# The low-rank gates of the odd layer: three 16-bit parts in one product of 96 rows, in place of rounded 4-byte parts in one of 80 rows

## The chip, the cores and the metric

The kernel runs on one core of one Trainium2 chip. The metric is the device time of one execution in microseconds; lower is better. The engines are called by the profile's names: PE is TensorE (PEld its weight loads), DVE is VectorE, ACT is ScalarE, POOL is GpSimd, and SP is SyncE, which here only issues DMAs.

## The reference, cut to what matters

One inference step of a decoder with two layers, for a prompt of 2048 tokens and 32 sample tokens (8 sequences of 4). Layer 0 has two head groups beside each other, a gated linear recurrence and a forgetting attention. Layer 1, the odd layer, is gated linear attention with four heads. Every layer ends with an output projection that is added to the input. What the change touches is the decay gate of the odd layer:

```python
proj = h @ w_in                                  # 1024 -> q 512, k 512, v 1024, g 1024, r 16
q, k, v, g, r = _split(proj, [...])
log_f = jax.nn.log_sigmoid((r @ w_gate + b_gate).astype(jnp.float32)) / GLA_GATE_NORMALIZER
...
o, s = gated_linear_chunked(hk(q) * C_KEY_DIM ** -0.5, hk(k), hv(v), hk(log_f), gla_s0)
```

The gate has rank 16: r has 16 columns per token, w_gate is 16 x 512, and each of the four heads uses 128 of the 512 columns. All inputs and outputs are float32.

## The kernel before, in words

Large projections are made with operands split in two float16 parts, high and low, and three products (`mm3`, lines 626 to 628: high x high, high x low, low x high). The tokens are worked off in two halves of 1024, the first with the 32 sample tokens behind it. A *unit* is a block of up to 272 output columns. For each unit the weights are loaded by SP into `wr_...`, measured, scaled by a power of two and split into `w_...` (`half_unit`, lines 338 to 366: L356 and L362/L363 on ACT, L357 on DVE, L364 on POOL); then the unit's own generator runs.

For each half of the odd layer there are three units a head: `mk_v` (values, and with head 0 the 16 columns of r), `mk_qk` (q, k and the gate), `mk_g` (the output gate). Beside the units of the next head or half runs `lin_attn` of the head before: the recurrence in levels of doubling width, with short products `gl_C` (L757) on PE, products of q, k and the running decay f on DVE (L789, L791) and POOL (L790), the sample tokens' step (`decode`, L796 to L846), and the outer products (`o_C`, `kt_C`). `mux` interleaves two generators in the program by costs written in the code. In the order that results, a scheduler of the framework (`schedule_with_timeline_sim=True`) then places the instructions of every engine's queue and gives tiles their buffers. `issue_after` adds an order without data.

The 16 columns of r take this way. In `mk_v` of head 0, for each group of 128 tokens (eight a half, and one of 32 in the first half), `ev` gets the projection in PSUM. ACT copies the values out (L1911). DVE makes `rh`, r scaled and rounded to the matrix engine's 4-byte format (L1920), copies it four times into `rt` (L1921) and puts the remainder in a fifth block of 16 columns (L1922). Two groups later `flip` transposes `rt` on PE into the PSUM tile `prT` (L1926), and DVE copies that into `rT` (L1927), 80 rows by 1024 or 1056 tokens. In `mk_qk`, `gate` multiplies the weights `wg` with `rT` in pieces of 352 columns (first half) or 512 (second) into the tile `zC` (L1951), 20 products in all, which ACT (L1953) and DVE (L1954) read.

`wg` is made once, in `more_consts`, which is placed early in the even layer (some 50 to 76 us into the span): a memset (L199), three loads of the same 16 rows to rows 0, 32 and 64 (L201), one rounding copy on ACT (L203), one subtraction on DVE (L204). The raw tile comes from the tag `y`, with three buffers, of which the tile `lb` (the even layer's lower bound, L175 to L194) also takes one, and out of which the five masks `mtmp` are made after it: a memset and two selects on POOL (L211, L213, L215) and four small casts on DVE each (L219). The first state loads of `lin_attn` (`s_A`, L830) use the same tag. In the same stretch the weights of the unit `Aqf` are scaled and split; L292 is the DVE instruction that reads a unit's maximum from the PSUM tile `spr_...` into `pow_...`.

Of the kernel before, what the change touches and what calls it, by code (L numbers as in the profile page):

```python
# [8 lines left out]
F32 = mybir.dt.float32  # L9
F32R = mybir.dt.float32r  # L10
BF16 = mybir.dt.bfloat16
# [3 lines left out]
AF = mybir.ActivationFunctionType  # L15
ALU = mybir.AluOpType
# [3 lines left out]
P = 128  # L20
# [3 lines left out]
HALF = 1024  # L24
DB, DS = 8, 4
TS = DB * DS
# [45 lines left out]
def as32(ap):  # L72

    return ap if ap.dtype == F16 else ap.bitcast(F32)
# [51 lines left out]
class Kern:  # L126
# [40 lines left out]
    def more_consts(self, mp):  # L167
        nc, i, cp, col = self.nc, self.i, self.cp, self.col
# [7 lines left out]
        l0, l1, m = (lb[:, r * NH : (r + 1) * NH] for r in range(3))  # L176
# [18 lines left out]
        self.bgla = col("bgla", i["b_gla_gate"][0], NH)  # L195


        wg = mp.tile([P, 512], F32, tag="y", name="wgr")
        nc.vector.memset(wg[:80], 0.0)  # L199
        for r in (0, 32, 64):  # L200
            nc.sync.dma_start(wg[r : r + 16], i["w_gla_gate"][0])  # L201
        self.wg = cp.tile([80, 512], F32R, name="wg")
        nc.scalar.activation(self.wg, wg[:80], AF.Copy)  # L203
        nc.vector.tensor_tensor(self.wg[32:48], wg[32:48], as32(self.wg[32:48]), ALU.subtract)  # L204
        self.bfox = cp.tile([P, NH], F32, name="bfox")
        nc.sync.dma_start(self.bfox, i["b_fox_f"].to_broadcast([P, NH]))

# [25 lines left out]
        for g in range(3):  # L233
            m = self.rowmask[g * TS : (g + 1) * TS]
# [1645 lines left out]
    def odd_half(self, hf, act, wpool, wp, pps, S):  # L1880
        nc, i, o = self.nc, self.i, self.o
        w = i["w_in_odd"][0]
        n = self.ncols(hf)
        q, f, k, v, vs, sg = {}, {}, {}, {}, {}, {}
        rTs = {}
        if hf == 0:
            self.q_undo = [self.kcol() for _ in range(NH)]

        def c4(nm):
            return wp.tile([P, HALF + TS], F32, tag="c4", name=nm)  # L1890

        def unit(n, h, run):
            nm, cols = self.odd_cols(h)[n]
            return (self.half_unit(wpool, pps, w, cols, f"{nm}{h}", f"{nm}{hf}{h}"), run)

        def undo(nm):
            return self.scales[nm][:, 2:3]

        def mk_v(h):
            width = 272 if h == 0 else 256  # L1900

            def run(W):
                v[h] = wp.tile([P, 8, 256], F32, tag="v8", name=f"vC{hf}{h}")
                vs[h] = wp.tile([TS, 256], F32, tag="vs", name=f"vsC{hf}{h}")
                if h == 0:
                    rTs[0] = wp.tile([80, HALF + TS], F32R, tag="rT", name=f"rT{hf}")

                def ev(ps, g, cnt, m):
                    c = undo(f"Cv{h}")[:m]
                    if m == P:  # L1910
                        r = nc.scalar.activation(v[h][:, g : g + cnt], ps[:, :, :256], AF.Copy, scale=c)  # L1911
                        if h == 0:
                            self.last_ev = r
                    else:
                        nc.scalar.activation(vs[h], ps[:, 0, :256], AF.Copy, scale=c)
                    if h == 0:
                        rt = wp.tile([P, 5, 16], F32, tag="rt", name=f"rt{hf}{g}")
                        rh = wp.tile([P, 16], F32R, tag="rh", name=f"rh{hf}{g}")
                        r = ps[:, 0, 256:272]
                        nc.vector.tensor_scalar(rh[:m], r, c, None, ALU.mult)  # L1920
                        nc.vector.tensor_copy(rt[:m, :4], as32(rh[:m]).unsqueeze(1).to_broadcast([m, 4, 16]))  # L1921
                        nc.vector.scalar_tensor_tensor(rt[:m, 4], r, c, as32(rh[:m]), ALU.mult, ALU.subtract)  # L1922

                        def flip():
                            pr = pps.tile([P, 512], F32, tag=PRT[hf], name=f"prT{hf}{g}")
                            nc.tensor.transpose(pr[:80, :m], rt[:m].rearrange("p a b -> p (a b)"), self.ident[:m, :m])  # L1926
                            nc.vector.tensor_copy(rTs[0][:, g * P : g * P + m], pr[:80, :m])  # L1927

                        if len(waiting) > 1:
                            waiting.pop(0)()  # L1930
                        waiting.append(flip)

                waiting = []
                yield from self.proj_tm(pps, act, W, hf, ev, f"Cv{hf}{h}", width)
                for x in waiting:
                    x()

            return unit(0, h, run)

        def mk_qk(h):  # L1940
            def run(W):
                nm = f"C{hf}{h}"

                def gate():
                    f[h], u = c4("f" + nm), c4("u" + nm)
                    ff = f[h]
                    for x, (c0, m) in enumerate(self.segs(hf)):
                        if x and h == 0:
                            yield
                        ps = pps.tile([P, 512], F32, tag="pj", name=f"z{nm}{c0}")  # L1950
                        nc.tensor.matmul(ps[:, :m], self.wg[:, h * P : (h + 1) * P], rTs[0][:, c0 : c0 + m],  # L1951
                                         start=True, stop=True)
                        nc.scalar.activation(ff[:, c0 : c0 + m], ps[:, :m], AF.Abs, bias=self.bgla[:, h : h + 1])  # L1953
                        nc.vector.tensor_scalar(u[:, c0 : c0 + m], ps[:, :m], self.bgla[:, h : h + 1], 0.0,  # L1954
                                                ALU.add, ALU.min)
                    nc.scalar.activation(ff[:, :n], ff[:, :n], AF.Exp, scale=-1.0)
                    nc.scalar.activation(ff[:, :n], ff[:, :n], AF.Ln, bias=1.0)
                    nc.vector.tensor_tensor(ff[:, :n], u[:, :n], ff[:, :n], ALU.subtract)
                    nc.scalar.activation(ff[:, :n], ff[:, :n], AF.Exp, scale=1.0 / 16)

                q[h], k[h] = c4("q" + nm), c4("k" + nm)
                c = undo(f"Cqk{h}")
                if hf == 0:
                    nc.vector.tensor_scalar(self.q_undo[h], c, SCALE, None, ALU.mult)
                yield from self.proj_fm(pps, act, W, 0, P, hf, lambda ps, c0, m: nc.scalar.activation(
                    q[h][:, c0 : c0 + m], ps, AF.Copy, scale=self.q_undo[h]), nm + "q")
                gates = gate()
                next(gates, None)
                yield Z_C
                for x in self.proj_fm(pps, act, W, P, P, hf, lambda ps, c0, m: nc.scalar.activation(  # L1970
                        k[h][:, c0 : c0 + m], ps, AF.Copy, scale=c), nm + "k"):
                    next(gates, None)
                    yield x

            return unit(1, h, run)

        def mk_g(h):
            def run(W):
                nm = f"C{hf}{h}"
                sg[h] = []  # L1980
                for t in range(2):
                    s = wp.tile([P, HALF + TS], F32, tag="sg", name=f"sg{t}{nm}")
                    sg[h].append(s)
                    yield from self.proj_fm(pps, act, W, t * P, P, hf, lambda ps, c0, m: self.silu2(
                        wp, s[:, c0 : c0 + m], ps, m, f"{nm}{t}{c0}", undo(f"Cg{h}")), f"{nm}g{t}")

            return unit(2, h, run)

        us = []
        for h in range(NH):  # L1990
            us += [mk_v(h), mk_qk(h), mk_g(h)]

        def lin(h):
            return self.lin_attn(wp, pps, hf, h, 256, q[h], f[h], k[h], v[h], vs[h], sg[h],
                                 self.g_gla[:, 2 * h : 2 * h + 2], S[h], i["state_gla"][0, :, h],
                                 o["gla_s"][0, :, h], o["gla_p"][0, 0, h],
                                 [self.yT[1][2 * h + t] for t in range(2)], f"C{hf}{h}")

        return us, lin
# [223 lines left out]
```

## Time and profile before

| | before |
|---|---|
| median of 3 runs | 2328.9 us |
| lowest and highest run | 2323.44 and 2330.65 us |
| profiled execution, its time | 2327.16 us |
| its span, first to last instruction | 2325.5 us |
| granted TensorE clock, mean | 0.991 |
| PE busy | 2251.2 us, 97% of the span |
| DVE, ACT, POOL busy | 1377.3, 1026.8, 727.0 us |

The span is what the trace covers; the execution's time is 1.7 us longer. In a row of the timeline stand the start, the duration, the engine, the line, the operation, the tile written and the tiles read, the shapes and the count; in brackets the time for which the engine was idle before it and what ended that. A row of waits names who waited for whom, then the sum, the number of times and the longest. A row of one tile or one line gives the shortest, median and longest duration in ns, and the first and last start in us. Ends of matmul records are modelled; starts are not. Records of the 4-byte product carry the type f32.

### The profile page before, as it was taken

The numbers are of one execution on the slowest core, as the hardware profiler recorded it, in microseconds if no ns is written. First come the engines' busy times: TensorE is split into PE (matmuls) and PEld (weight loads), VectorE is DVE, ScalarE is ACT, GpSimd is POOL, SyncE is SP. The second block draws the span as 40 slices with busy tenths as digits, with TensorE's granted clock in tenths as the row PEclk, the third lists the DMA queues.
The fourth block names the chain that finished last, engine by engine and source line by source line (L and its number), as shares of the span: only waits on it lengthen the run. The fifth ranks groups of instructions, "written<-read, shape, count | busy, mean of one in ns | idle before, by whom it ended". The sixth has DMA issues, their size and how long they took to land.

```text
span 2325.5 us, 57677 instructions
## 1 busy us (share of the span) xinstructions
PE 2251.2 (97%) x23060; PEld 1605.5 (69%) x23060; DVE 1377.3 (59%) x3074; ACT 1026.8 (44%) x2264; POOL 727.0 (31%) x780
## 2 busy tenths in 40 slices
PE   7999999999999999999999999999999999999998
PEld 5677678855755876655446888777677666666887
DVE  7756558525653657577767455366665655547554
ACT  6434354211212226456656543545544644554343
POOL 2223424001201214123335445144551432222232
PEclk9999999999999999999999999999999999999999
DMA  7343444755432378876972969424224431115553
GB/s 238 121 126 99 146 135 163 206 137 160 143 120 73 124 187 282 236 248 191 274 257 82 343 193 267 130 79 143 82 93 93 124 92 58 49 56 164 171 186 150
DMA packets 357422, 361.63 MB, mean 156 GB/s; under 512 B 105777, under 2 KB 300658, under 8 KB 353058
## 3 DMA queue, kind: packets, MB, share of 16 engines
q1 hardware_dynamic: 355010, 351.33, 49.3%
q0 software_dynamic: 2144, 6.62, 0.8%
q8 instruction: 181, 2.97, 0.5%
q14 instruction: 87, 0.71, 0.1%
HBM read 244.54 MB, written 96.42 MB: 147 GB/s over the span
## 4 chain that ended last, share of the span: by engine, by line
PE 42%; DVE 2%; POOL 2%; ACT 2%; DMA 1%; issue 1%; SPq 0%; POOLq 0%; DVEq 0%; ACTq 0%
PE pt_o L626 4%; PE pt_o L627 4%; PE pt_o L628 4%; PE pt_Cv L626 2%; PE pt_Cv L628 2%; PE pt_Cv L627 2%; PE gl_C L757 1%; PE o_C L910 1%; PE pt L1449 1%; PE pv L1711 1%; DMA yr<-yT 1%; POOL s_C L843 1%; PE py_C L729 1%; POOL kC L790 0%; PE fo L626 0%
## 5 line engine op out<-in xcount | busy, mean ns | idle before, releaser
L626 PE MATMUL pt_o<-w_o,act 128*128 128x256 f16 x1024 | 279.6, 273 | 2.7 <-ACT sg1C L683 2.7
L627 PE MATMUL pt_o<-w_o,act 128*128 128x256 f16 x1024 | 279.7, 273 | 0.0
L628 PE MATMUL pt_o<-w_o,act 128*128 128x256 f16 x1024 | 279.5, 273 | 0.1
L626 PEld LDWEIGHTS <-act 128*128 128x128 f16 x2304 | 226.3, 98 | 37.4 <-issue 3.7
L627 PEld LDWEIGHTS <-act 128*128 128x128 f16 x2304 | 226.4, 98 | 32.9 <-issue 4.2
L628 PEld LDWEIGHTS <-act 128*128 128x128 f16 x2304 | 226.4, 98 | 30.6 <-issue 2.0
L790 POOL TENSOR_TENSOR kA<-kA,fA 128x512 f32<-128x512 f32 (+1 forms) x56 | 77.2, 1378 | 339.5 <-PE gl_A L757 274.5
L626 PE MATMUL pt_Cv<-w_Cv,act 128*128 128x256 f16 (+1 forms) x512 | 141.4, 276 | 0.0
L627 PE MATMUL pt_Cv<-w_Cv,act 128*128 128x256 f16 (+1 forms) x512 | 141.3, 276 | 0.0
L628 PE MATMUL pt_Cv<-w_Cv,act 128*128 128x256 f16 (+1 forms) x512 | 141.3, 276 | 0.0
L1429 POOL TENSOR_SCALAR L<-L,nm 128x512 f32<-128x512 f32 (+3 forms) x160 | 99.3, 634 | 107.7 <-DVE nm L1425 41.5
L1421 ACT ACTIVATE L<-L,nm,kc 128x512 f32<-128x512 f32 (+3 forms) x160 | 118.2, 740 | 27.7 <-DVE nm L1419 26.9
L790 POOL TENSOR_TENSOR kC<-kC,fC 128x512 f32<-128x512 f32 (+1 forms) x56 | 80.2, 1433 | 142.2 <-PE gl_C L757 100.1
L1456 ACT ACTIVATE th<-pt 128x512 f16<-128x512 f32 (+3 forms) x159 | 81.8, 529 | 92.5 <-PE pt L1449 91.1
L1457 DVE TENSOR_TENSOR tl<-pt,th 128x512 f16<-128x512 f32 (+3 forms) x159 | 95.1, 609 | 21.2 <-ACT th L1456 19.5
L1449 PE MATMUL pt<-ident,L 128*128 128x128 f32 x544 | 91.8, 281 | 1.6 <-POOL L L1429 1.0
L1573 PEld LDWEIGHTS pkt<-ident,pgcache_fox_k 128*128 128x128 f32 x512 | 58.3, 141 | 44.0 <-issue 25.1
L789 DVE TENSOR_TENSOR qC<-qC,fC 128x512 f32<-128x512 f32 (+1 forms) x56 | 73.4, 1311 | 23.4 <-PE gl_C L757 23.4
L1449 PEld LDWEIGHTS pt<-ident,L 128*128 128x128 f32 x544 | 67.6, 144 | 26.1 <-DVE tl L1457 5.2
L1573 PE MATMUL pkt<-ident,pgcache_fox_k 128*128 128x128 f32 x512 | 77.7, 278 | 6.8 <-ACT kts L1577 2.5
L1911 ACT ACTIVATE vC<-pt_Cv,kc 128x512 f32<-128x512 f32 (+1 forms) x40 | 23.9, 599 | 136.5 <-PE pt_Cv L628 136.5
L789 DVE TENSOR_TENSOR qA<-qA,fA 128x512 f32<-128x512 f32 (+1 forms) x56 | 70.1, 1253 | 12.5 <-PE gl_A L757 12.4
(959 smaller groups left out, 6558.2 us busy)
## 6 DMA issues: line engine op xcount, KB each, us to landing
pgcache_fox_k<-in_cache_fox_k SPq DMA_DIRECT2D x128, 256.0 KB, 4.2
pgcache_fox_v<-in_cache_fox_v SPq DMA_DIRECT2D x128, 256.0 KB, 4.1
yr<-yT SPq DMA_DIRECT2D x16, 1024.0 KB, 6.8
x1d<-xo SPq DMA_DIRECT2D x44, 256.0 KB, 3.6
wr_o<-in_w_out_even SPq DMA_DIRECT2D x32, 256.0 KB, 5.1
xo<-in_x_prompt SPq DMA_DIRECT2D x32, 256.0 KB, 5.6
wr_Cv<-in_w_in_odd SPq DMA_DIRECT2D x32, 256.0 KB, 3.5
x1r<-x1d SPq DMA_DIRECT2D x16, 512.0 KB, 4.2
```

Source lines behind the costliest of these rows:

```text
L626: nc.tensor.matmul(ps, lh[0], rh[0], start=first, stop=False)
L627: nc.tensor.matmul(ps, lh[0], rh[1], start=False, stop=False)
L628: return nc.tensor.matmul(ps, lh[1], rh[0], start=False, stop=last)
L789: nc.vector.tensor_tensor(xv[:, :, 1], xv[:, :, 1], t0.to_broadcast([P, nb, w]), ALU.mult)
L790: nc.gpsimd.tensor_tensor(kv[:, :, 0], kv[:, :, 0], t1.to_broadcast([P, nb, w]), ALU.mult)
L1421: self.last_exp = nc.scalar.activation(lt[:, :w], lt[:, :w], AF.Exp, bias=nm[:, 0:1], scale=ib, accum_out=nm[:, 2 + j : 3 + j])
L1429: nc.gpsimd.tensor_scalar(lt[:, :w], lt[:, :w], nm[:, 1:2], 2.0**14, ALU.mult, ALU.mult)
L1449: nc.tensor.transpose(pt[:, w : w + P], rows[b][s // 4][0][:, (s % 4) * P : (s % 4 + 1) * P], self.ident)
L1456: nc.scalar.activation(th[:, a:w], pt[:, a:w], AF.Copy),
L1457: nc.vector.tensor_tensor(tl[:, a:w], pt[:, a:w], th[:, a:w], ALU.subtract)))
L1573: last = nc.tensor.transpose(pk[:, j * P : (j + 1) * P], pgs[j][:, h * P : (h + 1) * P], self.ident)
L1911: r = nc.scalar.activation(v[h][:, g : g + cnt], ps[:, :, :256], AF.Copy, scale=c)
```

## The change

Both operands of the gate's product are split into three bfloat16 parts, in place of a rounded part and a remainder. Six blocks of 16 rows, 96 in all, hold the parts 0, 1, 2, 0, 1, 0 of the weights against the parts 0, 0, 0, 1, 1, 2 of r, so that one product sums the six pairs. The weights' parts are made by two ACT copies and two DVE subtractions on 16 rows and are put in place by six DMAs of 16 KB that POOL issues, where before the rows came from HBM three times and were computed in place. For r, DVE makes the high part (16 bits), the remainder, its 16-bit part, three copies of the first and two of the second, and subtracts once more. `rT` holds 16-bit values in a tile of the same size as before.

```diff
@@ more_consts
-        wg = mp.tile([P, 512], F32, tag="y", name="wgr")
-        nc.vector.memset(wg[:80], 0.0)
-        for r in (0, 32, 64):
-            nc.sync.dma_start(wg[r : r + 16], i["w_gla_gate"][0])
-        self.wg = cp.tile([80, 512], F32R, name="wg")
-        nc.scalar.activation(self.wg, wg[:80], AF.Copy)
-        nc.vector.tensor_tensor(self.wg[32:48], wg[32:48], as32(self.wg[32:48]), ALU.subtract)
+        wg, left = (mp.tile([P, 512], F32, tag="y", name=x)[:16] for x in ("wgr", "wgl"))
+        nc.sync.dma_start(wg, i["w_gla_gate"][0])
+        w3 = mp.tile([P, 512], F32, tag="pd", name="wg3")
+        parts = [w3[:16, 0:256].bitcast(BF16), w3[:16, 256:512].bitcast(BF16), mp.tile([P, 512], F32, tag="kt", name="wg1")[
+            :16, :256].bitcast(BF16)]
+        self.wg = cp.tile([96, 512], BF16, name="wg")
+        nc.scalar.activation(parts[0], wg, AF.Copy)
+        nc.vector.tensor_tensor(left, wg, parts[0], ALU.subtract)
+        nc.scalar.activation(parts[1], left, AF.Copy)
+        nc.vector.tensor_tensor(parts[2], left, parts[1], ALU.subtract)
+        for g, x in enumerate((0, 1, 2, 0, 1, 0)):
+            nc.gpsimd.dma_start(self.wg[16 * g : 16 * g + 16], parts[x])
@@ mk_v
-                    rTs[0] = wp.tile([80, HALF + TS], F32R, tag="rT", name=f"rT{hf}")
+                    rTs[0] = wp.tile([P, HALF + TS], F32, tag="rT", name=f"rT{hf}").bitcast(BF16)[:96, : HALF + TS]
...
-                        rt = wp.tile([P, 5, 16], F32, tag="rt", name=f"rt{hf}{g}")
-                        rh = wp.tile([P, 16], F32R, tag="rh", name=f"rh{hf}{g}")
+                        rt = wp.tile([P, 6, 16], F32, tag="rt", name=f"rt{hf}{g}")
+                        rh = wp.tile([P, 2, 16], BF16, tag="rh", name=f"rh{hf}{g}")
                         r = ps[:, 0, 256:272]
-                        nc.vector.tensor_scalar(rh[:m], r, c, None, ALU.mult)
-                        nc.vector.tensor_copy(rt[:m, :4], as32(rh[:m]).unsqueeze(1).to_broadcast([m, 4, 16]))
-                        nc.vector.scalar_tensor_tensor(rt[:m, 4], r, c, as32(rh[:m]), ALU.mult, ALU.subtract)
+                        nc.vector.tensor_scalar(rh[:m, 0], r, c, None, ALU.mult)
+                        nc.vector.scalar_tensor_tensor(rt[:m, 5], r, c, rh[:m, 0], ALU.mult, ALU.subtract)
+                        nc.vector.tensor_copy(rh[:m, 1], rt[:m, 5])
+                        nc.vector.tensor_copy(rt[:m, :3], rh[:m, 0:1].to_broadcast([m, 3, 16]))
+                        nc.vector.tensor_copy(rt[:m, 3:5], rh[:m, 1:2].to_broadcast([m, 2, 16]))
+                        nc.vector.tensor_tensor(rt[:m, 5], rt[:m, 5], rt[:m, 3], ALU.subtract)
 
                         def flip():
                             pr = pps.tile([P, 512], F32, tag=PRT[hf], name=f"prT{hf}{g}")
-                            nc.tensor.transpose(pr[:80, :m], rt[:m].rearrange("p a b -> p (a b)"), self.ident[:m, :m])
-                            nc.vector.tensor_copy(rTs[0][:, g * P : g * P + m], pr[:80, :m])
+                            nc.tensor.transpose(pr[:96, :m], rt[:m].rearrange("p a b -> p (a b)"), self.ident[:m, :m])
+                            nc.vector.tensor_copy(rTs[0][:, g * P : g * P + m], pr[:96, :m])
```

## The prediction

> **What bounds the kernel now.** I read the first part of the page, then the chain that ended last, then TensorE's waits in the odd layer, then busy time in the two stretches in which the changed code runs.
>
> ```profile
> span 2325.5 us, 57677 instructions
> PE 2251.2 (97%) x23060; PEld 1605.5 (69%) x23060; DVE 1377.3 (59%) x3074; ACT 1026.8 (44%) x2264; POOL 727.0 (31%) x780
> PE 42%; DVE 2%; POOL 2%; ACT 2%; DMA 1%; issue 1%; SPq 0%; POOLq 0%; DVEq 0%; ACTq 0%
> ```
>
> TensorE is busy for 97% of the span, and it is the engine with by far the most of the last chain. Work on the other engines costs time only where TensorE waits for it. In the odd layer those waits are few:
>
> ```profile
> PE gl_C L757 <- POOL kC L790: 5.2, 3, 1.8
> PE gl_C L757 <- DVE qC L711: 1.9, 1, 1.9
> PE o_C L626 <- ACT pd_C01s L861: 1.6, 1, 1.6
> PE ktS_C L805 <- DVE kr_C L804: 0.7, 1, 0.7
> PE gl_C L757 <- DVE qC L789: 0.3, 1, 0.3
> 1450.00:1483.00 33.00, 33.00 (x281) 25.48 (x280) 12.12 (x44) 15.85 (x31) 5.03 (x5) 1.00 0.76 192
> 1795.00:1830.00 35.00, 34.00 (x583) 24.12 (x581) 29.70 (x67) 16.85 (x37) 21.07 (x17) 1.00 0.72 174
> ```
>
> The last two rows are the stretches in which the rows of r are made, for the first and the second half of the tokens (columns: PE, PEld, DVE, ACT, POOL busy). In the first VectorE has 21 us free. In the second it has 5.3 us free, because the last head of the first half is worked off beside it, and POOL is busy for 21.07 of 35 us.
>
> **The change, part by part.** *The gate product.* There are twenty products zC, twelve of 352 columns and eight of 512. Their inputs become 16 bits wide and 96 rows deep.
>
> ```profile
> L1951 PEld LDWEIGHTS zC<-rT,wg x20: 186/190/193, 1483.6 to 2076.5; 80*128 80x128 f32 x20
> L1951 PE MATMUL zC<-rT,wg x20: 322/442/587, 1483.6 to 2076.8; 80*128 80x352 f32 x12, 80*128 80x512 f32 x8
> 1483.25 0.31 PE L626 MATMUL pf_C00q<-act,w_Cqk 128*128 128x352 f16 x1
> 1483.40 0.31 PE L627 MATMUL pf_C00q<-act,w_Cqk 128*128 128x352 f16 x1
> 1483.55 0.31 PE L628 MATMUL pf_C00q<-act,w_Cqk 128*128 128x352 f16 x1
> 1483.58 0.45 PE L1951 MATMUL zC<-rT,wg 80*128 80x352 f32 x1
> 1483.87 0.33 PE L626 MATMUL pf_C00k<-act,w_Cqk 128*128 128x352 f16 x1
> 1484.03 0.31 PE L627 MATMUL pf_C00k<-act,w_Cqk 128*128 128x352 f16 x1
> 1913.22 0.38 PE L627 MATMUL pf_C11q<-act,w_Cqk 128*128 128x512 f16 x1
> ```
>
> What the next product feels is the distance of starts, not the record's length. 16-bit products of 352 columns start 0.15 us apart. From the last of them (1483.55) over zC to the next (1483.87) are 0.32 us for two products, where two 16-bit ones take 0.30. So zC already runs at about the 16-bit rate, and the gain is 0.02 us each, 0.4 us for twenty. The other end is the records' own difference: 0.45 against 0.31 for 352 columns and, by the longest, 0.59 against 0.38 for 512, 12 x 0.14 + 8 x 0.21 = 3.4 us. I take 0.4, since starts are measured and ends modelled. The weight load (190 ns) already lies beside the product before it.
>
> [...]
>
> *The transposes.* Seventeen of 80 columns become 96 wide:
>
> ```profile
> L1449 PEld LDWEIGHTS pt<-ident,L 128*128 128x128 f32 x544 | 67.6, 144 | 26.1 <-DVE tl L1457 5.2 <-issue 4.4 <-POOL L L1429 2.4
> L1926 PEld LDWEIGHTS prT<-ident,rt 128*80 128x80 f32 x16 | 1.9, 118 | 1.4 <-DVE hl_C L807 0.4 <-issue 0.3 <-DVE rT L1927 0.2
> ```
>
> Between 118 ns at 80 and 144 ns at 128 columns the load grows by some 9 ns (an estimate from these two rows): 0.15 us for seventeen, between nothing and 17 x 26 ns = 0.4. The eviction L1927 has as many columns as before.
>
> *The rows of r on VectorE.* Three instructions a group become six, for nine groups in the first half and eight in the second.
>
> ```profile
> 1451.92 0.23 DVE L1920 TENSOR_SCALAR rh<-pt_Cv,kc 128x16 fp32r<-128x16 f32 x1 [2.54 <-ACT vC L1911]
> 1452.19 0.20 DVE L1921 COPY rt<-rh 128x64 f32<-128x64 f32 x1
> 1452.30 0.23 DVE L1922 SCALAR_TENSOR_TENSOR rt<-pt_Cv,kc,rh 128x16 f32<-128x16 f32 x1
> ```
>
> An instruction that reads what the one before it wrote starts 0.27 us after it (L1921), one that does not 0.11 us (L1922). The old three take 0.61 us. The new six are: hi part; remainder (+0.27); its cast to 16 bits (+0.27); copy of three groups (+0.11); copy of two groups (+0.16, waits for the cast); last subtraction (+0.27, and 0.23 of its own). That is 1.31 us, so 0.70 more a group, 11.9 us for all. The bank of the projection is read by the first two alone, so it comes free 0.1 us earlier than now. In the first half, 9 x 0.70 = 6.3 us go into 21 free us and cost nothing: the transposes run two groups (5.6 us) behind. If that cover were gone, they would be late by at most 0.7 us each. In the second half 8 x 0.70 = 5.6 us meet 5.3 us of free VectorE. Queued behind these instructions are L804 and L789 of the last head, on which TensorE already waits for 0.7 and 0.3 us. The floor is nothing (the order there can move them behind L789), the ceiling is 5.6 us. I take 1.5: one group's 0.70 in front of each of the two places where VectorE is late already, rounded up. Nothing else that VectorE does in this stretch stands in the list of TensorE's waits.
>
> *The setup, from 50 to 76 us.* ScalarE and VectorE do two instructions each instead of one each and a memset; SP issues one load instead of three; POOL gets six DMAs; one more buffer of tag y (three exist) is taken before the five masks are made in the same buffers.
>
> ```profile
> L199 DVE MEMSET wgr<- x1: 485/485/485, 62.0 to 62.0; 80x512 f32 x1
> L203 ACT ACTIVATE wg<-wgr x1: 632/632/632, 65.3 to 65.3; 80x512 fp32r<-80x512 f32 x1
> L204 DVE TENSOR_TENSOR wg<-wgr,wg x1: 682/682/682, 67.5 to 67.5; 16x512 fp32r<-16x512 f32 x1
> L1474 POOL DMA_DIRECT2D yT<-fy x17: 557/588/647, 875.4 to 1280.7; - x17
> 66.89 0.15 POOL L211 MEMSET mtmp<- 128x64 f32 x1 [14.81 <-DVE mlev L219]
> L213 POOL TENSOR_SCALAR_AFFINE_SELECT mtmp<-mtmp x5: 255/560/667, 50.7 to 71.1; 128x64 f32<-128x64 f32 x5
> L215 POOL TENSOR_SCALAR_AFFINE_SELECT mtmp<-mtmp x5: 308/625/650, 51.4 to 71.4; 128x64 f32<-128x64 f32 x5
> SPq L830 <- DVE mlev L219: 9.3, 2, 6.4
> SPq L201 <- DVE wgr L199: 8.3, 1, 8.3
> 71.87 2.65 DVE L219 CAST mlev<-mtmp 32x16 int8<-32x16 f32 x4
> L219 DVE CAST mlev<-mtmp x20: 153/170/1116, 65.8 to 76.1; 32x16 int8<-32x16 f32 x20
> 72.04 2.26 POOL L364 TENSOR_TENSOR w_Aqf<-wr_Aqf,w_Aqf 128x512 f16<-128x512 f32 x2
> 74.55 0.29 DVE L292 TENSOR_REDUCE pow_Aqf<-spr_Aqf 128x1 f32<-128x128 f32 x1
> 74.89 0.31 PE L626 MATMUL pf_A00f<-act,w_Aqf 128*128 128x352 f16 x1 [1.78 <-DVE pow_Aqf L292]
> ```
>
> VectorE: plus 2 x 0.68, minus 0.68 and 0.49, so 0.2 us; ScalarE plus 0.63; SP is freed of a wait of 8.3 us; what SP then holds up is L830, which waits for the masks' buffers and not for a free queue. POOL: 6 x 0.588 = 3.5 us, part of them in the 14.81 us before 66.89, when POOL has nothing to do. Here TensorE does wait: 1.78 us, because L292, which frees a bank, stands behind four mask casts of 2.65 us: a cast takes 0.17 us at the median, and up to 1.12 here, beside POOL's L364. Masks made one buffer later move this meeting. At best it goes (minus 1.8 us); then the split L364 is next, ready at 74.3. At worst the six DMAs and one mask (0.15 + 0.56 + 0.63 = 1.3 us) stand before L364: plus 4.9 us. I take plus 0.5, nearer to no change than to either end, because POOL's DMAs have idle time before them and the masks do not. What SP issues after L830, the next weights' loads, is costed at nothing, since no wait for them is on TensorE's side of these rows; if they are late after all, they are late by the masks' delay, which is in the 4.9 us already.
>
> The sum: -0.4 + 0.15 + 1.5 + 0.5 = +1.75 us. The profiled execution took 2327.2 us (a span of 2325.5 and 1.7 around it), which lies 1.7 us below the median of the three runs shown, 2328.9. Profile against profile I expect 2328.9; against the median 2330.7. Runs of this kernel spread over 7.2 us, so about 0.3% (7 us) is what can be told from no change.
>
> **The rivals.** *VectorE is held up by POOL in the second half (slower).* Four instructions a group work from SBUF to SBUF, where there was one. Each can be blocked as the longest mask cast was, by 0.95 us (1.12 - 0.17). With POOL busy for 60% of that stretch: 8 groups x 3 more instructions x 0.6 x 0.95 = 13.7 us, with 5.6 of their own and 5.3 free that is up to 14 us; at half of the blocking +7 us and with the other terms 2338. It decides from some 0.45 us of blocking an instruction. For it:
>
> ```profile
> L789 DVE TENSOR_TENSOR qC<-qC,fC x6: 678/1390/1808, 1798.7 to 1825.9; 128x512 f32<-128x512 f32 x4, 128x528 f32<-128x528 f32 x2
> L1921 DVE COPY rt<-rh x8: 195/196/422, 1795.3 to 1823.3; 128x64 f32<-128x64 f32 x8
> ```
>
> L789 takes up to 1.81 us in this stretch, where it can take 0.68. Against it: the one small copy that is there already took 196 ns at the median of eight, and 422 at most. [...] I give this 0.20.
>
> *The setup wait grows to its worst:* +4.9 instead of +0.5, 2335. It needs the order DMAs, masks, split on POOL. 0.12; it is within 0.3%.
>
> *The order is planned anew (faster).* All queues are written by a scheduler that sees other durations. The three waits at the top of the odd layer's list, 5.2 + 1.9 + 1.6 = 8.7 us, hang on when POOL and ScalarE come to kC and pd relative to TensorE; with these gone 2322, with the setup's 1.8 us too 2320. Nothing in the rows says that they would all go together. 0.15.
>
> [...] 0.03.
>
> **How the numbers follow.** No change to be measured: 0.50 for the sum and 0.12 for the worse setup, 0.62. Faster: 0.15 + 0.03 = 0.18. Slower: 0.20. Predicted is the sum, 2330.7. The likeliest case alone lies within 2326 and 2335 (the bounds of its terms, -3.4 - 1.8 and +5.6 - 1, not all at once). The range reaches to the other cases, 2320 at the faster ones and 2338 at the middle of the slower one; what lies beyond is the upper half of that rival, 0.1, and some of the faster ones, under 0.1.
>
> **What would show it.** zC in the profile after with records near 0.31 and 0.38 us, and some 0.30 us from the 16-bit product before it to the one after: the first term is right. [...] TensorE's wait at L804 and L789 near 1800 to 1830 should be 2 to 3 us instead of 1.0. At 75 us, the wait of pf_A00f between 0 and 7 us tells which setup it was. Wrong would be the prediction if the waits for kC and pd in the odd layer changed by more than 5 us in sum, or if TensorE gained more than 3 us at zC.

## The result and the profile after

| | before | after |
|---|---|---|
| median, lowest and highest run (9 runs each) | 2326.57 us, 2321.73 to 2330.65 | 2335.62 us, 2333.35 to 2338.49 |
| ratio after to before, 95% interval | | 1.0045, 1.0035 to 1.0054 |
| profiled execution, span, mean granted clock | 2327.16, 2325.5, 0.991 | 2335.69, 2334.0, 0.990 |

The change costs 9 to 10 us. The time lies inside the range of the prediction, but 4.9 us above the predicted one, and the likeliest forecast, no change to be measured, did not come true. That it lies inside the range is in part luck: the range reached up to 2338 for the sake of a rival whose price did not come about as it was reckoned.

The head of the page after, its chain, and the two stretches in which the rows of r are made, placed by the same work as those of before, the first 1 us longer (columns as before):

```profile
span 2334.0 us, 57742 instructions
PE 2256.1 (97%) x23060; PEld 1606.4 (69%) x23060; DVE 1384.6 (59%) x3125; ACT 1027.9 (44%) x2265; POOL 731.0 (31%) x786
PE 37%; DVE 3%; DMA 2%; ACT 2%; POOL 1%; issue 1%; SPq 1%; POOLq 0%; DVEq 0%; ACTq 0%
1454.00:1488.00 34.00, 34.00 (x287) 26.07 (x285) 17.04 (x71) 15.88 (x31) 4.64 (x4) 1.00 0.80 198
1803.00:1838.00 35.00, 32.06 (x566) 23.24 (x564) 32.45 (x88) 13.45 (x29) 18.61 (x15) 0.95 0.70 171
```

TensorE is still the bound. In the first stretch it is busy all the time. In the second it loses 2.94 of 35 us (before: 1.00), VectorE is busy for 32.45 us in place of 29.70, and the column of the granted clock has fallen from 1.00 to 0.95: TensorE not only waited, it ran slower for part of the stretch. Its busy time over the span rose by 4.9 us, although the products cost less than before: the slow ones are counted in it, with records of 0.50 us in place of 0.31 behind the wait at 75 us (below). TensorE's waits in the odd layer:

```profile
PE gl_C L762 <- POOL kC L795: 5.5, 4, 1.8
PE o_C L631 <- ACT pd_C00s L866: 2.4, 1, 2.4
PE gl_C L762 <- DVE qC L794: 2.2, 1, 2.2
PE gl_C L762 <- DVE qC L716: 1.9, 1, 1.9
PE o_C L631 <- ACT pd_C01s L866: 1.6, 1, 1.6
PE ktS_C L810 <- DVE rt L1926: 0.7, 1, 0.7
```

Two are new or grown: qC in the last head of the first half (L789 before, L794 now) from 0.3 to 2.2 us, and pd_C00s. Outside the odd layer, after and, in the second fence, a further execution of the kernel before (`before_again` below), from 60 to 86 and 855 to 915 us:

```profile
PE pf_A00f L631 <- DVE pow_Aqf L297: 2.3, 1, 2.3
PE psf L1628 <- ACT lfTs L1627: 2.4, 2, 2.0
PE pkt L1578 <- ACT kts L1582: 0.3, 1, 0.3
```

```profile
PE pf_A00f L626 <- DVE pow_Aqf L292: 1.8, 1, 1.8
PE psf L1623 <- ACT lfTs L1622: 0.8, 2, 0.6
PE pkt L1573 <- ACT kts L1577: 1.2, 1, 1.2
```

At 75 us the setup's wait is 0.5 us longer; at 908 us there is a wait of 2.0 us for the sums of the forget gates, in a part of the kernel that no edited line touches.

What such a wait costs is more than its length. TensorE's timeline at its end, in the setup and in the odd layer (start, duration, engine, line):

```profile
74.68 0.45 PE L631 MATMUL pf_A00f<-act,w_Aqf 128*128 128x352 f16 x1 [2.27 <-DVE pow_Aqf L297]
...
75.22 0.50 PE L631 MATMUL pf_A00f<-act,w_Aqf 128*128 128x352 f16 x1
75.51 0.50 PE L632 MATMUL pf_A00f<-act,w_Aqf 128*128 128x352 f16 x1
...
78.20 0.31 PE L633 MATMUL pf_A00f<-act,w_Aqf 128*128 128x352 f16 x1
78.35 0.31 PE L631 MATMUL pf_A00f<-act,w_Aqf 128*128 128x352 f16 x1
```

```profile
1821.57 0.28 PE L633 MATMUL pt_Cv<-w_Cv,act 128*128 128x272 f16 x1
1821.69 0.28 PE L631 MATMUL pt_Cv<-w_Cv,act 128*128 128x272 f16 x1
...
1824.31 0.73 PE L762 MATMUL gl_C<-qC,kC 128*32 128x16 f32 x64 [2.23 <-DVE qC L794]
...
1825.85 0.43 PE L633 MATMUL pt_Cv<-w_Cv,act 128*128 128x272 f16 x1
1826.08 0.43 PE L631 MATMUL pt_Cv<-w_Cv,act 128*128 128x272 f16 x1
```

Equal products start 0.29 us apart behind the first wait and 0.15 us later on; behind the second, 0.23 in place of 0.12. Half clock (a granted clock of 0.5) lasts 3.41 us in eleven places of this profile and 6.83 us in one, its end left aside, and with products twice as far apart 3.41 us of it cost up to 1.7 us of work (an estimate). In the profile after it stands at or just behind the waits at 75, 418, 861, 908, 1568 and 1824 us, among others; these are 2.3, 2.1, 2.7, 2.0, 2.4 and 2.2 us long.

So the loss can be laid along the span. Start of a TensorE product in single executions, in us for `before_again` and as the distance to it for the others (`after_again` is a second execution of the changed kernel, the last three are experiments below):

| product (first, if not said) | before_again | before | after | after_again | rows_16bit | dmas_on_sp | sp_16bit |
|---|---|---|---|---|---|---|---|
| pf_A00q, behind the setup's wait | 85.8 | +0.1 | +1.4 | +2.7 | 0.0 | -1.9 | -2.8 |
| spr_o, before the forgetting attention | 438.6 | -1.2 | +3.1 | +2.5 | +1.6 | -1.5 | -2.6 |
| pkt, last, at the end of the forgetting attention | 1068.2 | -0.1 | +6.4 | +4.9 | +3.0 | -1.5 | -2.0 |
| pf_C01q, last | 1558.5 | +3.5 | +6.3 | +5.5 | +3.6 | +0.6 | -3.6 |
| pf_C01g | 1578.3 | +1.0 | +8.3 | +7.2 | +5.3 | +0.2 | -3.7 |
| oS_C, last, before the last head's wait | 1812.1 | +1.0 | +8.9 | +10.1 | +4.2 | +1.4 | -2.5 |
| pf_C10q, behind it | 1820.9 | +1.0 | +12.4 | +12.8 | +3.7 | +4.8 | -3.0 |
| pt_o, last | 2312.9 | +3.8 | +12.2 | +18.9 | +5.4 | +7.1 | 0.0 |

After loses 1.4 us in the setup, 1.7 on the way to spr_o (half clock behind a wait of 2.1 us at 418 us, where `before_again` waits 1.9 us without it), 3.3 in the forgetting attention, 2.0 at 1565 us and 3.5 beside the last head: 11.9 of 12.2 us. In `after_again` the setup costs 2.7 us, the way to spr_o nothing, the forgetting attention 2.4, the place at 1565 us 1.7 and the last head 2.8; the other losses of its 18.9 us have no counterpart in the profile after. Such single steps are uncertain: between the two executions of the kernel before they differ by up to 2.8 us, and once by 3.6.

### The profile page after: what moved, and what is told of

It is laid out like the page before. It is cut to its first block, busy times and chain, and to the rows that moved or that the text cites. A ratio compares the mean times of both kernels' runs of the same rounds, so it can differ in the third digit from the quotient of the medians.

```text
span 2334.0 us, 57742 instructions
## 1 busy us (share of the span) xinstructions
PE 2256.1 (97%) x23060; PEld 1606.4 (69%) x23060; DVE 1384.6 (59%) x3125; ACT 1027.9 (44%) x2265; POOL 731.0 (31%) x786
## 5 line engine op out<-in xcount | busy, mean ns | idle before, releaser
L794 DVE TENSOR_TENSOR qC<-qC,fC 128x512 f32<-128x512 f32 (+1 forms) x56 | 73.9, 1320 | 21.9 <-PE gl_C L762 21.9
L794 DVE TENSOR_TENSOR qA<-qA,fA 128x512 f32<-128x512 f32 (+1 forms) x56 | 70.1, 1251 | 12.5 <-PE gl_A L762 12.4
```

Source lines behind the costliest of these rows:

```text
L794: nc.vector.tensor_tensor(xv[:, :, 1], xv[:, :, 1], t0.to_broadcast([P, nb, w]), ALU.mult)
```

## The experiments

Theory A: the largest single loss is the row part, VectorE beside the last head. Theory B: it is what the setup did to the order of the rest. Ratios are to the kernel before on the same chip; the 1.0045 of the changed kernel was measured ahead of the experiments and not again beside them, so a comparison with it assumes that it holds there too.

**Two more executions**, to see what repeats. 

> The kernel before, profiled a second time, to see which waits and which half-clock stretches of TensorE belong to the program and which come and go. Theory A (the row part): the stretches outside the wait at L789 near 1814 us come and go by 3.4 us each, but the setup up to 340 us falls within 0.3 us of the first profile, and the wait at 1814 us is again under 0.6 us. Theory B (the re-planned order costs): everything up to 2100 us falls as in the first profile within 1 us.

> The changed kernel, profiled a second time. Theory A: at 340 us it is again 1.3 to 1.4 us behind the kernel before; the gl_C wait near 1824 us is again 2 us or more with half clock behind it, so 3 to 4 us are lost there; the half-clock stretches at 419 and 1569 us need not return. Theory B: the losses of 2 us near 420 and of 4 us near 1565 us are there again, since the order is the same.

They took 2323.41 and 2342.47 us; the second is 4 us above the highest of the nine runs of the changed kernel. The kernel before fell as theory A forecast in the setup (0.1 us apart) and in the last head (a wait of 0.3 us again), and up to 3.5 us apart elsewhere, against theory B. In the changed kernel the wait for qC came again with 2.2 us, but without the half clock that was forecast behind it; the one at 908 us came again with 2.0 and that for pd_C00s with 2.3, both with half clock. The loss of the setup was to repeat with 1.3 to 1.4 us; it was 2.7, by a longer wait:

```profile
PE pf_A00f L631 <- DVE pow_Aqf L297: 3.8, 1, 3.8
```

The wait for pd_C00s at 1565 us stands in `before_again` too, with 2.0 us but no half clock behind it, and not in the first execution of before. Ahead of pd, ScalarE scales a weight and waits for its DMA before that: 1.90 us in the profile after, 1.56 in `before_again`, 0.48 in before. So most of that wait is not the change's.

**The row part alone, in the kernel before.** Three more instructions a group, and nothing else:

```diff
+ rb = rt[:, 1, :8].bitcast(BF16)
+ nc.vector.tensor_copy(rb[:m], rt[:m, 4])
+ nc.vector.tensor_copy(rt[:m, 3], rb[:m])
+ nc.vector.tensor_tensor(rt[:m, 3], rt[:m, 4], rt[:m, 3], ALU.subtract)
```

The results stand in blocks of r that meet zero rows of the weights, so the gate's sum stays as it was. 

> The kernel before, with three instructions more a group on VectorE (a cast of the remainder to 16 bits, a copy of it back, a subtraction), whose results meet zero rows of the weights. Setup, gate product and the order of everything else are those of before. Theory A (the row part is the largest loss, because these instructions wait for POOL beside the last head of the first half): 2.5 to 4.5 us slower than before, and a gl_C wait of 2 us or more near 1815 us. Theory B (the loss is spread by the new setup and plan): 0 to 1.5 us slower, the wait under 1 us.

Measured: 2328.18 us, 1.0013 (0.9998 to 1.0027): 3.0 us, as theory A forecast, but the interval holds no change as well. TensorE's wait in the last head:

```profile
PE gl_C L757 <- DVE qC L789: 2.2, 1, 2.2
```

It is the wait of the changed kernel, with half clock behind it (1817.0 us), and TensorE loses 3.5 us there in total.

**The change without the row part.** The lower parts of r are left out: one copy into five places takes the place of the four instructions.

```diff
- nc.vector.tensor_copy(rh[:m, 1], rt[:m, 5])
- nc.vector.tensor_copy(rt[:m, :3], rh[:m, 0:1].to_broadcast([m, 3, 16]))
- nc.vector.tensor_copy(rt[:m, 3:5], rh[:m, 1:2].to_broadcast([m, 2, 16]))
- nc.vector.tensor_tensor(rt[:m, 5], rt[:m, 5], rt[:m, 3], ALU.subtract)
+ nc.vector.tensor_copy(rt[:m, :5], rh[:m, 0:1].to_broadcast([m, 5, 16]))
```

> The changed kernel with three instructions a group on VectorE, as before; the two lower parts of r are left out, with copies of the high part in their place. Theory A: 3 to 5 us faster than the changed kernel, so 4 to 6 us above before (setup 1.4 us and the rest). Theory B: within 1.5 us of the changed kernel, 7.5 to 10.5 us above before.

Measured: 2332.09 us, 1.0023 (1.0009 to 1.0037); the wait for qC is gone from the list. That is 6.9 us above before, between theory A's 4 to 6 and theory B's 7.5 to 10.5. So the row part is worth some 0.002, and another 0.002 lies elsewhere: neither theory is enough.

**The weights' remainder in another buffer.** In the changed kernel the masks come one buffer later in their tag; here they don't.

```diff
- wg, left = (mp.tile([P, 512], F32, tag="y", name=x)[:16] for x in ("wgr", "wgl"))
+ wg, left = (mp.tile([P, 512], F32, tag=t, name=x)[:16] for t, x in (("y", "wgr"), ("kt", "wgl")))
```

> The changed kernel with the remainder of the gate's weights in a buffer of another tag, so that the buffers of the five masks are taken in the order of the kernel before. Theory B (setup): the wait of pf_A00f near 74 us falls from 2.27 to below 1.8 us, without the stretch at half clock behind it, TensorE is level with before at 86 us (it was 1.4 to 2.6 us behind in two profiles of the changed kernel), and the time falls by 1.4 to 2.6 us, to about 1.0037 of before. Theory A: POOL's six DMAs alone hold the masks up; the wait stays at 2.0 us or more, and the ratio at 1.0045.

Measured: 2335.46 us, 1.0037 (1.0021 to 1.0053). The setup's wait fell, and TensorE was level with `before_again` at 86 us:

```profile
PE pf_A00f L631 <- ACT fA L1000: 0.9, 1, 0.9
```

That is B's profile and B's 1.0037, but the interval of the time holds 1.0045 as well: 1.4 us can't be told in the time. In this profile the gain did not last: at spr_o TensorE is 3.4 us behind again, after half clock behind a wait of 2.3 us at 418 us.

**r written as 16-bit parts straight from PSUM**, four VectorE instructions a group, of which only the last has all its inputs in SBUF; the transposes go through a 16-bit identity, which POOL copies once at 3 us:

```diff
+ r1 = ps[:, 0:1, 256:272]
+ nc.vector.tensor_scalar(rt[:m, :3], r1[:m].to_broadcast([m, 3, 16]), c, None, ALU.mult)
+ nc.vector.scalar_tensor_tensor(rh[:m], r, c, rt[:m, 0], ALU.mult, ALU.subtract)
+ nc.vector.scalar_tensor_tensor(rt[:m, 3:5], r1[:m].to_broadcast([m, 2, 16]), c, rt[:m, 0:2],
+                                ALU.mult, ALU.subtract)
+ nc.vector.tensor_tensor(rt[:m, 5], rh[:m], rt[:m, 3], ALU.subtract)
...
+ nc.tensor.matmul(pr[:96, :m], rt[:m].rearrange("p a b -> p (a b)"), self.identb[:m, :m],
```

> The changed kernel with the six groups of r written as 16-bit numbers straight from the projection's bank: four VectorE instructions a group (hi part into three places; remainder in 4 bytes; middle part into two places; low part), of which three read PSUM and only the last reads two tiles of SBUF; the transposes then go through a 16-bit identity. Theory A (row part: about 3.5 us of the loss come from small instructions of SBUF alone that POOL's work beside the last head of the first half stretches, and from the half clock that TensorE gets after the long wait for qC there): that wait falls from 2.2 us to below 1 us, no half-clock stretch at 1820 to 1830, the groups of r take 1 us or less, and the time is 3 to 4 us below that of the changed kernel: 1.0030 of before in place of 1.0045. Theory B (the rows are not it; the new order in the setup and the later stretches is): 1.0045 again, within 0.001.

Measured: 2330.3 us, 1.0019 (1.0006 to 1.0031). Of TensorE's waits from 1795 to 1840 us one is left, as long as before:

```profile
PE ktS_C L812 <- DVE kr_C L811: 0.7, 1, 0.7
```

Theory A's forecast, and more than it: 0.0026 less than the changed kernel, some 6 us. Not all of this has to be the rows: in this profile the setup's wait for pow_Aqf is 1.4 us in place of 2.3, without half clock, and TensorE is level with `before_again` at 86 us. The edit does not touch this stretch. VectorE's part of the split of w_Aqf, which stands in its queue just before the instruction that ends the wait, began at 72.75 us, 0.1 us before POOL's part, and took 0.75 us; in the profile after it began at 72.82 us, 0.1 us behind POOL's, and took 1.61.

**Both edits together.** 

> Both edits together: rows of r as 16-bit numbers straight from the projection's bank, and the weights' remainder in the other buffer. If both parts of the loss are what they seem (3.5 us beside the last head, 1.4 to 2.6 us in the setup) the ratio to before is 1.0020, 4.5 us above it, and what stays is the wait of head 0's o_C for ScalarE's pd near 1565 us (2.3 us and the half clock behind it, 4 us). If that wait is a matter of where TensorE's half-clock stretches happen to lie and not of the program, it is absent in some of the profiles and the ratio is nearer to 1.0005.

Measured: 2329.51 us, 1.0019 (1.0006 to 1.0032). The buffer added nothing to the rows that the time shows. Nor did it mend the setup here: TensorE waits there twice, 1.1 us for POOL's w_Aqf and 0.9 for fA, and is 1.2 us behind `before_again` at 86 us. The wait for pd_C00s is absent in this profile, and the ratio is not the 1.0005 that was forecast for that case, so what stays, 0.0019, is not that wait alone.

**The cast and the two copies on ScalarE** (`nc.scalar.activation(..., AF.Copy)` in the three places). 

> The changed kernel with the cast of the middle part and the two copies into the groups made by ScalarE; VectorE keeps three instructions a group, the number it had before. Theory A: VectorE has its old load beside the last head again; the wait for qC falls below 1 us and the ratio goes from 1.0045 to 1.0030, if ScalarE's 17 x 3 small instructions, two hand-overs between the engines a group, do not hold up its pd and kT work by as much. Theory B: 1.0045 or, by ScalarE's extra 17 x 0.7 us beside the heads, up to 1.006.

Measured: 2331.18 us, 1.0027 (1.001 to 1.0043): theory A's 1.0030 lies within the interval, theory B's 1.0045 just outside. The wait for qC is gone, and part of it has come back as a wait for rT:

```profile
PE prT L1934 <- DVE rT L1935: 1.1, 2, 0.8
```

**The six copies of the weights' parts issued by SP.**

```diff
- nc.gpsimd.dma_start(self.wg[16 * g : 16 * g + 16], parts[x])
+ nc.sync.dma_start(self.wg[16 * g : 16 * g + 16], parts[x])
```

With this one word the scheduler writes the forgetting attention in the order of the kernel before. Between the first spr_o and the last pkt, 149 of TensorE's 5838 products stand in another order than before in each of the eight profiles in which POOL issues the copies, and none does where SP issues them. 

> The changed kernel with the six small copies that fill the gate's weights issued by SP and not by POOL; nothing else is edited. With them on POOL the planned order of the forgetting attention (860 to 910 us) differs from that of the kernel before; with them on SP it is that of the kernel before again. Theory A (the row part is the largest loss, the new order costs nothing): the wait for the sums of the forget gates at 908 us goes, but the time stays at 1.0045 within 0.001. Theory B (the new order costs a 2.0 us wait at 908 us with half a clock for 3.4 us behind it, against 1.8 us of waits that it saves, so about 2 us, and POOL's copies in the setup 1.4 us): no half-clock stretch near 908 us in the profile, TensorE level with before at 86 us, and the ratio falls by 3 to 3.5 us, to 1.0030.

Measured: 2328.15 us, 1.0018 (1.0009 to 1.0028), below the changed kernel's interval and below theory B's 1.0030. The waits outside the odd layer:

```profile
PE pf_A00f L631 <- ACT fA L1000: 0.9, 1, 0.9
...
PE psf L1628 <- ACT lfTs L1627: 0.8, 2, 0.6
PE pkt L1578 <- ACT kts L1582: 1.2, 1, 1.2
```

The 2.0 us at 908 us and the half clock behind them are gone. Each of the eight profiles with the copies on POOL has both; of the six others (three of the kernel before, with and without more row instructions, and three with the copies on SP) none has either. In the table above the stretch from spr_o to the end of pkt costs 3.3 us more than in `before_again` in the kernel after, 1.4 more in `rows_16bit`, which has the same order there, and nothing more in this one; the eight profiles lie between 1.4 and 3.4 us. The setup contributes as much: the wait of 1.8 us for pow_Aqf that before has is gone too, only 0.9 us for fA are left, and TensorE is 1.9 us ahead of `before_again` at 86 us, 3.3 us ahead of after. Theory B's place, then, is the order planned anew and the setup together; the times do not separate the two, and part of the 0.0027 is a gain over before and no loss undone.

**Both parts mended:** r from PSUM, and the copies on SP. 

> Both edits that the two theories call for: r's groups as 16-bit numbers straight from the projection's bank (1.0019 alone) and the six copies on SP. If the losses add up (3 us by SP's copies, 4 to 6 us by the rows, of some 10 in all), the ratio is 1.0000 to 1.0010, and what stays is the wait of head 0's o_C near 1565 us. If the planned order is not where the rest lies: 1.0019 again.

Measured: 2323.12 us against 2322.94, 0.9999 (0.9988 to 1.0009). The losses add up: 0.0026 and 0.0027 where each is mended alone, 0.0046 together, equal to their sum within the intervals, and nothing of the 0.0045 is left. Against `dmas_on_sp`, on the same chip, the rows are worth 5.0 us. The zero holds a gain, though: in this profile TensorE is 2.8 us ahead of `before_again` behind the setup's wait. It is the better version of the change, and no faster than the kernel before.

**Form or amount?** Two more instructions that read PSUM and write nothing new are added to each group, on POOL's and then on SP's copies:

```diff
+ nc.vector.scalar_tensor_tensor(rh[:m], r, c, rt[:m, 1], ALU.mult, ALU.subtract)
+ nc.vector.scalar_tensor_tensor(rh[:m], r, c, rt[:m, 2], ALU.mult, ALU.subtract)
```

> The kernel with r's groups as 16-bit numbers straight from the projection's bank, and two more VectorE instructions a group that write nothing new (the remainder made twice more, each reading the bank): six instructions a group, the number of the changed kernel, 34 more than without them, but only one of the six with SBUF alone for its inputs. Theory A1 (what hurts is the form: instructions of SBUF alone are held up beside POOL): the extra two take 0.2 us each, the wait for qC near 1820 us stays under 1 us, and the ratio stays at 1.0019 to 1.0025. Theory A2 (what hurts is the amount of work on a VectorE that had 5.3 us free in that stretch): the wait for qC is back at 2 us or more, with the half clock behind it, and the ratio is 1.0035 to 1.0045.

> The same question again on a quieter ground: the kernel with both edits (four VectorE instructions a group, six copies on SP; 0.9999 of before), and the two more instructions a group that read the projection's bank and write nothing new. Against the kernel with the copies on SP alone (1.0018) it has as many instructions a group, six, but of the six one and not four work on SBUF alone. Theory A1, the form: 1.0000 to 1.0005, and the wait for qC near 1815 us under 1 us with no half clock behind it. Theory A2, the amount: 1.0018 again. Between the two, 1.0009 to 1.0012: both have a part, the amount through VectorE's queue in front of qC and prT, the form through the stretched instructions and a wait long enough to bring the half clock.

Measured: 2331.18 us, 1.0041 (1.0028 to 1.0055), and 2327.42 us, 1.0010 (0.9998 to 1.0022). On POOL's copies the time is that of theory A2 and the wait that of A1: 0.9 us for qC, without half clock. What costs the further 0.0022 over `rows_16bit` there is not shown. On SP's copies the time is the value between the theories, and its interval holds the forecasts of both. With what was measured above:

| rows of r, VectorE instructions a group | copies by POOL | copies by SP |
|---|---|---|
| six, four of them on SBUF alone (the change's) | 1.0045 | 1.0018 |
| six, one of them on SBUF alone | 1.0041 | 1.0010 |
| four, one of them on SBUF alone | 1.0019 | 0.9999 |

Both columns put the larger share on the amount (0.0022 and 0.0011) and the smaller on the form (0.0004 and 0.0008), but each interval is 0.001 wide to either side: that the amount costs something is likely, the form's share is not settled by the times. The traces show a wait of each kind. The rows of the second kernel, durations in ns, and its waits in the last head (`pt_Cv` is a tile of PSUM; `few_Cv`, the projection of the sample tokens, is put together in SBUF):

```profile
L1934 DVE TENSOR_TENSOR rt<-rh,rt x17: 159/175/807, 1446.8 to 1821.2; 128x16 bf16<-128x16 f32 x16, 32x16 bf16<-32x16 f32 x1
L1929 DVE SCALAR_TENSOR_TENSOR rh<-pt_Cv,kc,rt x16: 223/234/235, 1445.8 to 1819.2; 128x16 f32<-128x16 f32 x16
L1929 DVE SCALAR_TENSOR_TENSOR rh<-few_Cv,kc,rt x1: 1117/1117/1117, 1473.2 to 1473.2; 32x16 f32<-32x16 f32 x1
...
PE gl_C L764 <- DVE qC L796: 0.7, 1, 0.7
PE prT L1938 <- DVE rT L1940: 0.5, 1, 0.5
PE prT L1938 <- DVE rt L1934: 0.2, 1, 0.2
```

The instructions that read PSUM never took more than 269 ns, the one on SBUF alone up to 807. The same line, L1929, took at most 235 ns in the sixteen groups that it reads from PSUM, and 1117 in the one that it reads from SBUF, beside POOL's split of w_Cv (1472.37 us, for 1.89). The amount leaves waits of 0.7 and 0.5 us without half clock; with the stretched forms there is one of 2.2 us in each of five profiles, in four of them with it.

## Why the prediction missed the loss, step by step

**The gate product: right.** 0.02 us each were forecast by the distance of starts, and none of the 3.4 us of the records' lengths:

```profile
1487.12 0.31 PE L633 MATMUL pf_C00q<-act,w_Cqk 128*128 128x352 f16 x1
1487.27 0.31 PE L1959 MATMUL zC<-rT,wg 96*128 96x352 bf16 x1
1487.42 0.31 PE L631 MATMUL pf_C00k<-act,w_Cqk 128*128 128x352 f16 x1
```

From the product before zC to the one after it are 0.30 us, 0.32 before. That the records would shrink to 0.31 while the time does not was the reading that held. For the 0.03 among the chances of a faster kernel no run shows a ground: the 4-byte product cost 0.02 us more than the 16-bit one.

**The transposes: right.** The median load of `prT` went from 118 to 126 ns.

**The rows of r: the place was right, the cost not.** The sum had 1.5 us for it, one group's 0.70 at each of two late places. An undisturbed group takes 1.12 us in the profile after (1803.03 to 1804.15), less than the 1.31 worked out. Yet TensorE loses 2.8 to 3.5 us around this wait in the five profiles with six instructions a group, four of them on SBUF alone, and by the ratios the rows cost 0.0013 (added to the kernel before) to 0.0026 (mended in the changed one, perhaps with some of the setup in it), 3 to 6 us: the upper half of the span from nothing to 5.6 us. The rival that had VectorE held up by POOL named what was missing. VectorE, then POOL, in the stretch of the wait:

```profile
1816.73 0.17 DVE L1927 CAST rh<-rt 128x16 bf16<-128x16 f32 x1
...
1818.40 1.27 DVE L1927 CAST rh<-rt 128x16 bf16<-128x16 f32 x1
1819.59 2.13 DVE L823 TENSOR_TENSOR kpad_C<-hl_C,rowmask 96x512 fp32r<-96x512 f32 x2
1821.64 1.01 DVE L1929 CAST rt<-rh 128x32 f32<-128x32 bf16 x1
1822.68 0.29 DVE L773 COPY_PREDICATED dg<-mlev,gl_C 128x128 f32<-128x128 int8 x1
1822.88 1.28 DVE L794 TENSOR_TENSOR qC<-qC,fC 128x512 f32<-128x512 f32 x1
...
1818.37 1.27 POOL L795 TENSOR_TENSOR kC<-kC,fC 128x512 f32<-128x512 f32 x1
1819.60 5.47 POOL L848 TENSOR_TENSOR s_C<-s_C,fC 128x512 f32<-128x512 f32 x4
```

A cast of 16 columns that takes 0.17 us takes 1.27 beside POOL's kC of 1.27, the next 1.01 beside s_C, and qC's product stands behind both. Two stretched casts, not the rival's fourteen (8 x 3 x 0.6), delay this product. They took 1.9 us more than the same casts undisturbed, and by 1.9 us the wait for qC grew, to a length behind which TensorE mostly got half clock (in four of five profiles). The instructions of these groups that read PSUM took 235 ns at most in this profile. The rival's 7 us for half of the blocking was the sum of many small delays; the runs showed a few, and a clock. Its 2338 also counts the rows twice, since 2338 is 7 us on top of 2330.7, which holds 1.5 for them already: 2336.2 would be the sum. That the measured 2335.6 lies near it is luck, as a good part of the loss came from elsewhere. The waits at the two places were forecast at 2 to 3 us together and are 2.9, but by another way: that of ktS_C did not grow (0.7 us), and qC alone went from 0.3 to 2.2. The step that was left out is the clock behind a wait of that length.

**The setup: the wait came out in one profile, its consequence was not in the sum.** 0.5 us more was forecast for the wait of pf_A00f, and 0.5 was measured in the first profile (1.8 to 2.3 us), but 2.0 in the second (3.8), so the agreement is in part luck; 1.4 and 2.7 us were lost by 86 us. The clock has a share in it: of three profiles with a wait of 2.3 us, after and `three_row_ops` had half clock with it and were 1.4 and 1.8 us late, `copies_on_act` had none and was 0.2 late. That POOL's copies would have idle time before them was half right: three stand in such time at 48 us, but the first mask's memset moved from 50.5 to 61.3 us, behind the remainder's subtraction. This move alone does not make the wait: in `left_in_kt` and `dmas_on_sp`, which wait 0.9 us there, the memset starts at 61.4 and 61.1 us.

**Nothing was put on the order of other stages, other than as a gain.** The rival of an order planned anew was in the text, as a way to be faster. It came, by the copies on POOL, and it was slower: 2.0 us at 908 us with half clock, 1.4 to 3.4 us in the profiles. With the setup this is the 0.0027 that the copies on SP take away. The signs at which the prediction would be called wrong, the waits for kC and pd_C in the odd layer, grew by 2.7 us in sum (2.4 of them at 1565 us, told above), less than the 5 us named.

## What to carry to other kernels

Where the bound engine is busy for 97%, price a wait by what it does to that engine's clock too: here one of 2.0 to 2.3 us mostly cost up to 1.7 us more, those under 1 us in the last head nothing more, so shortening such a long wait is likely worth more than its length. Half clock came behind short waits close together too: from 1167.6 to 1175.6 us of the profile before TensorE is busy for 5.92 of 8 us, with no wait over 0.9 us, and half clock follows at 1175.6 us. Small instructions on a second engine are to be counted, and read from PSUM where they can be, when a third engine streams SBUF beside them: here those of r's rows took 270 ns at most from PSUM (`rows_16bit`), and up to 1273 on SBUF alone (the profile after). With a planned order, look at the queues that result even for stages that the edit doesn't touch: six small DMAs issued by POOL changed an order and so made a wait 850 us later, and giving them to SP was worth as much as rewriting the computation.

## What the runs showed of the hardware that was not expected

- Half clock lasted 3.41 us, or twice that, wherever it ended within the span, and it begins at another distance from the same wait in each execution: 0.8 us behind the wait at 908 us in the profile after, 0.4 in `after_again`. Behind waits of 2.0 to 2.4 us it came in most cases but not all: behind one of 2.10 us at 418 us it did in the profile after, behind one of 2.23 us at the same place it did not in `after_again`; behind the wait of 2.2 us for qC it did in the first and not in the second.
- That may account for part of the spread of a kernel's own runs (2319.25 to 2334.73 us in 23 runs of the kernel before): two profiles of that kernel hold 40 and 21 us at half clock within the span. Half of the difference would be 10 us, but their spans differ by 3.8, so not every such stretch cost the 1.7 us of the estimate.
- The 4-byte product zC of the rounded format cost TensorE about what its 16-bit form does: 0.32 us from the product before it to the one after it in the profile before, 0.30 in the one after, at 352 columns.
